# Three input projections by seven block products in place of eight, and modulations computed in other phases

## The chip, the cores and the metric

The program runs on one core of a Trainium2 chip, in one launch. The metric is the device time of that core in microseconds. The kernel before takes 2531.38 us in the median of three runs (2527.74 to 2532.80). The profile and the trace come from one more execution of 2533.03 us, whose first and last instructions lie 2531.3 us apart (the span); all times below are counted from the first instruction of the span. TensorE is named PE in the rows, VectorE DVE, ScalarE ACT, GpSimd POOL and SyncE, which issues the transfers, SP.

## The reference

Two layers on a stream of 512 tokens with 1024 features, plus 256 context tokens. Each layer is half an FFN, a token mixer (HGRN in layer 0, a gated MLP over chunks in layer 1), and half an FFN. Every part is modulated before it and normalised behind it:

```python
def swiglu(h, w_in, w_out):
    gate, up = jnp.split(h @ w_in, 2, axis=-1)
    return (jax.nn.silu(gate) * up) @ w_out

def macaron_half_ffn(x, m, k, w_in, w_out, g, b):
    return post_norm_update(x, 0.5 * swiglu(modulate(x, m, k), w_in, w_out), m, k, g, b)

def modulate(x, m, k):
    return x * (1 + m[..., 3 * k + 1, :]) + m[..., 3 * k, :]

def post_norm_update(x, y, m, k, g, b):
    return layer_norm(DN_ALPHA * x + m[..., 3 * k + 2, :] * y, g, b)
```

`m` holds nine vectors of 1024 for each layer, silu(condition) times a matrix of 1024 x 9216. The hidden width of an FFN is 2816, that is 22 slices of 128, and each slice has a gate half and an up half. All of it is float32.

## The kernel before, in words

**Products.** A float32 operand is kept as two parts: a high part that ScalarE rounds off (L130) and a low part that VectorE subtracts (L131). `mm3` (L140 to L144) makes a product of three matmuls: high by high (L142), high by low (L143), low by high (L144). A weight is loaded as a `unit` (L133) of 128 x 1024: a transfer into `raw` (three buffers), then a split into `w` (six buffers).

**An FFN** is an input phase and an output phase. `FeedIn.rest` (L457) goes over the slices of the hidden width. For each it takes two units, gate and up. Each unit is eight slices of the 1024 features, and each slice multiplies a 128 x 128 block of weights with all 512 tokens: 48 matmuls of 512 columns for the pair, into two PSUM banks `psf`. ScalarE then takes silu of the gate bank (L452), VectorE multiplies it with the up bank (L454) to `h`. f0, f2, f3 and f4 are such phases over the 512 tokens, f1 is one over the 256 context tokens (`psf<-xmc`, 256 columns).

**Output and transition.** `OutPhase` multiplies `h`, split into `hs`, with the output weights into the banks `y`, one half of the 1024 features after the other. Behind the second half comes the transition: VectorE adds the residual and takes statistics (`evac`, L293 to L298), normalises (`norm`), TensorE transposes to banks `pt`, the modulation is applied there in place (L334, L336), and a split writes the next operand `xm` (`operand`). While these steps run, the next phase already multiplies its first two pairs, slice by slice, on 256 tokens at a time (`staged`, four units); `rest` does the other 20 pairs. `store` (L284 to L286) then scales each of the four row tiles by the gain row `rg` and adds the offset row `rb`, for one half of the features and then for the other, and writes them to memory; the rows of the second half are loaded over those of the first, once the latter have been used.

**Modulations.** A vector of `m` is eight chunks of 128 x 1024 loaded into `mraw` (two buffers, L170), each with two VectorE operations (`junk<-mraw,srow_x`, L164). They stand in a queue of generators. `mod_step` takes some at certain places of the loops and `made` takes what is missing. (l;ch) below is vector ch of layer l; ch 2, 5 and 8 are gates, written to memory as rows. (0;8) and (1;2) are queued before f2's rest, (1;5), (1;7), (1;6) and (1;8) before f3's.

**Order.** A planner sorts the instructions of each engine's queue by its own estimates; each queue then runs strictly in that order, so that an instruction that waits holds all that stand behind it on its engine. `tc.issue_after` in the transition holds store() back until the last operand's split has been placed. All transfers shown here are issued from one queue, SyncE's. Pools of SBUF tiles are opened and closed from phase to phase; a tile of a new pool may lie over tiles of an old one, and its first writer then waits for the old one's last users.

Of the kernel before, what the change touches and what calls it, by code (L numbers as in the profile page):

```python
# [70 lines left out]
def backbone_kernel(  # L71
# [36 lines left out]

    last = ctx.enter_context(tc.tile_pool(name="last", bufs=1, side="right"))
# [30 lines left out]
    def mm3(ps, a, b, start, stop):  # L140
        (ah, al), (bh, bl) = a, b
        nc.tensor.matmul(ps, ah, bh, start=start, stop=False)  # L142
        nc.tensor.matmul(ps, ah, bl, start=False, stop=False)  # L143
        return nc.tensor.matmul(ps, al, bh, start=False, stop=stop)  # L144
# [83 lines left out]
    class OutPhase:  # L228
# [4 lines left out]
        def __init__(self, hget, nk, units, nt, l, j, cond, yscale, xsrc, scaled, after, xm, xdst, nxt, tail=2):  # L233
            self.hget, self.nk, self.units, self.nt, self.tail = hget, nk, units, nt, tail
            self.l, self.j, self.cond, self.yscale, self.xsrc = l, j, cond, yscale, xsrc
            self.scaled, self.after, self.xm, self.xdst, self.nxt = scaled, after, xm, xdst, nxt
            self.npair, self.bp = nk // 2, None
            self.ys, self.pos = [[], []], [0, 0]

        def operands(self, hf, kk):  # L240
            w = unit(self.units(hf, kk))
            n, hs = self.nt * P, []
            for i in range(2):
                h = self.hget(2 * kk + i)
                if h.dtype != F32R:
                    s = self.bp.tile([P, 2, T], F32R, tag="hs", name="hs", bufs=2 * self.tail)
# [72 lines left out]
        def operand(self, p, kb):  # L319

            o, ks = slice(p * 2 * P, (p + 1) * 2 * P), slice(2 * kb, 2 * kb + 2)
            cols, xm = self.cols, self.xm
            pt = bank("pt").rearrange("p (k t) -> p k t", t=2 * P)
            for i in range(2):
                k = 2 * kb + i
                for t in range(2):
                    nc.tensor.transpose(
                        pt[:, i, t * P : (t + 1) * P], self.xs[2 * p + t][:, k * P : (k + 1) * P], ident
                    )
            for i in range(2):  # L330
                k = 2 * kb + i
                g, b = cols[:, 0, k : k + 1], cols[:, 1, k : k + 1]
                if i:
                    nc.scalar.activation(pt[:, i, :], pt[:, i, :], AF.Identity, scale=g, bias=b)  # L334
                else:
                    nc.vector.tensor_scalar(pt[:, i, :], pt[:, i, :], g, b, ALU.mult, ALU.add)  # L336
            return split(xm[:, 0, ks, o], xm[:, 1, ks, o], pt)

        def run(self, bp, hook=None, nmod=0):
# [21 lines left out]
            for t in range(nt):  # L361
                for h in held:
                    self.part(1, *h, [t])

# [12 lines left out]
            for i in range(len(steps) + 3):  # L377
                if i == 1 and nt > 2:
                    done(1)
                if i:  # L380
                    nxt.ahead(i)
                if i < len(steps):
                    last = self.operand(*steps[i])
                if i >= 3:
                    nxt.staged(*steps[i - 3])
            if self.xdst is not None:
# [22 lines left out]
    class Phase:  # L409
# [6 lines left out]

        @staticmethod
# [10 lines left out]
    class FeedIn(Phase):  # L428


# [18 lines left out]
        def evac(self, hp, psg, psu):  # L449
            n = self.n  # L450
            s = hp.tile([P, T], F32, tag="silu", name="silu", bufs=1)
# [5 lines left out]
        def rest(self, hp, nmod):  # L457
# [12 lines left out]
            for _ in self.later:  # L470
                pass
            return lambda k: self.hs[k]
# [59 lines left out]
    with sbuf(name="hp", bufs=1) as hp, sbuf(name="modp", bufs=1) as modp:  # L532
# [49 lines left out]
        with bpools() as bp:  # L582

            def context_operand():
# [6 lines left out]
                for ch in (5, 7, 6):  # L591
                    queue_mod(modp, srow, 0, ch, ["x"])
# [15 lines left out]
            ).run(bp)  # L608
# [3 lines left out]
    with sbuf(name="hgo", bufs=1) as hgo, ExitStack() as late:  # L612
# [14 lines left out]
        with sbuf(name="hg", bufs=1) as hg:  # L627
# [234 lines left out]
            f2 = FeedIn(0, 1, None, NT)  # L862
# [51 lines left out]
        with bpools() as bp:  # L914
            xm = new_xm(xmp, "xm", T)
            f2.xm = op.xm = xm
            op.run(bp)
# [3 lines left out]
    with sbuf(name="hp2", bufs=1) as hp, sbuf(name="modp2", bufs=1) as modp, bpools() as bp:  # L921
        srow = {"x": silu_row(modp, "x")}
# [4 lines left out]
        f3 = FeedIn(1, 0, xm, NT)  # L927
        OutPhase(
            hget, NF, ffn_units(0, 1), NT, 0, 2, "x", 0.5, lambda t: x2[t], True, (1, 0),
            xm, lambda t: x3[t], f3, tail=3,  # L930
        ).run(bp, None, 1)
        for ch in (5, 7, 6, 8):
            queue_mod(modp, srow, 1, ch, ["x"])
        hget = f3.rest(hp, 1)
# [27 lines left out]
        OutPhase(  # L962
            hget, NF, ffn_units(1, 0), NT, 1, 0, "x", 0.5, lambda t: x3[t], True, (1, 1),
            xm, lambda t: x4[t], first, tail=3,
        ).run(bp, None, 1)
        for ch in (5, 7, 6, 8):
            made((1, ch, "x"))


    with ExitStack() as vhp_stack:  # L970
# [3 lines left out]
        f4 = FeedIn(1, 1, None, NT)  # L974
# [4 lines left out]
        op.bp = bp  # L979
        with sbuf(name="cm", bufs=1) as cm:  # L980
# [6 lines left out]
            for gi in range(NG):  # L987
# [4 lines left out]
                for t in range(NT):  # L992
                    if gi == 0:
                        ps = first.ps[t]
                    else:
                        ps = bank("pscv")
                        cm_tok(ps, xm, ws, t)
                    nc.scalar.activation(vt[:, t, :], ps[:, :GC], AF.Gelu_apprx_tanh)
                    nc.vector.bn_stats(st[t][:, gi, :], vt[:, t, :])
            stat = []  # L1000
# [47 lines left out]
    with sbuf(name="hp4", bufs=1) as hp, bpools() as bp:  # L1048
        hget = f4.rest(hp, 0)
# [82 lines left out]
```

## Time and profile before

| | |
|---|---|
| median of three runs | 2531.38 us (2527.74 to 2532.80) |
| the profiled execution | 2533.03 us |
| its span | 2531.3 us |
| TensorE busy | 2484.4 us, 98% |
| VectorE busy | 1551.8 us, 61% |
| ScalarE busy | 892.1 us, 35% |
| rest of f2, f3, f4 | 1026.7 to 1244.4, 1394.9 to 1612.4, 2184.5 to 2401.9 us |
| first output phase (layer 0, first FFN) | 260 to 373 us |
| HGRN mixer | 608 to 994 us |
| loop of the chunk MLP's gate | 1747 to 1872 us |

In the table of engines the first number is the busy time, then its share of the span and the instructions. A row of the groups gives line, engine, operation, output<-inputs, shape and count, then the busy time, the mean ns of one, the idle time of the engine just before them and what ended most of it. A row of the timeline is start, length, engine, line, operation, and in brackets the idle time just before with its releaser; xN behind it joins N rows that follow one another. A row of the windows gives the stretch, its length, then busy time and starts of each engine, the granted clock of TensorE (1.00 is full), the busy share of the DMA engines and GB/s. Matmuls overlap, so the distance of their starts, not their listed duration, is what one costs in a full queue.

### The profile page before, as it was taken

The numbers are of one execution on the slowest core, as the hardware profiler recorded it, in microseconds if no ns is written. First come the engines' busy times: TensorE is split into PE (matmuls) and PEld (weight loads), VectorE is DVE, ScalarE is ACT, GpSimd is POOL, SyncE is SP. The second block draws the span as 40 slices with busy tenths as digits, with TensorE's granted clock in tenths as the row PEclk, the third lists the DMA queues.
The fourth block names the chain that finished last, engine by engine and source line by source line (L and its number), as shares of the span: only waits on it lengthen the run. The fifth ranks groups of instructions, "written<-read, shape, count | busy, mean of one in ns | idle before, by whom it ended". The sixth has DMA issues, their size and how long they took to land.

```text
span 2531.3 us, 31944 instructions
## 1 busy us (share of the span) xinstructions
PE 2484.4 (98%) x12527; PEld 2130.6 (84%) x12527; DVE 1551.8 (61%) x2773; ACT 892.1 (35%) x1227; POOL 45.9 (2%) x82
## 2 busy tenths in 40 slices
PE   7999999999999999999999999999999999999998
PEld 5888789988788888888888888888998888888887
DVE  7987668575888886766356432357376356632255
ACT  4222335463445442322243322344232233422241
POOL 0000000000000000000000000000000000000001
PEclk9999999999999999999999999999999999999999
DMA  8878436655521113787232522223443222532221
GB/s 325 287 251 273 154 104 208 197 191 192 193 83 59 59 59 121 253 276 256 96 102 85 185 93 99 99 86 123 160 139 101 83 92 92 189 103 97 95 93 57
DMA packets 111144, 367.70 MB, mean 145 GB/s; under 512 B 12760, under 2 KB 16016, under 8 KB 110992
## 3 DMA queue, kind: packets, MB, share of 16 engines
q1 hardware_dynamic: 110992, 365.65, 42.9%
q8 instruction: 98, 1.61, 0.3%
q14 instruction: 54, 0.44, 0.1%
HBM read 352.99 MB, written 12.61 MB: 144 GB/s over the span
## 4 chain that ended last, share of the span: by engine, by line
PE 74%; DVE 14%; DMA 7%; issue 2%; ACT 2%; POOL 1%; SPq 0%; DVEq 0%; POOLq 0%
PE psf L143 12%; PE psf L144 12%; PE psf L142 11%; PE y L144 8%; PE y L142 8%; PE y L143 8%; DMA mraw<-in_mod_w 6%; DVE junk L164 3%; DVE w L131 2%; PE pscv L143 2%; PE pscv L144 2%; PE pscu L143 2%; PE pscu L142 2%; PE pscv L142 2%; PE pscu L144 2%
## 5 line engine op out<-in xcount | busy, mean ns | idle before, releaser
L131 DVE TENSOR_TENSOR w<-raw,w 128x1024 fp32r<-128x1024 f32 (+1 forms) x458 | 550.2, 1204 | 323.2 <-ACT w L130 321.3
L130 ACT ACTIVATE w<-raw 128x1024 fp32r<-128x1024 f32 (+1 forms) x458 | 473.5, 1039 | 456.2 <-PE psf L144 217.9
L142 PE MATMUL psf<-xm,w 128*128 128x512 f32 (+1 forms) x1504 | 565.9, 378 | 18.4 <-ACT xm L130 17.9
L143 PE MATMUL psf<-xm,w 128*128 128x512 f32 (+1 forms) x1504 | 567.6, 378 | 2.0 <-DVE xm L131 2.0
L144 PE MATMUL psf<-xm,w 128*128 128x512 f32 (+1 forms) x1504 | 567.1, 377 | 2.2 <-DVE w L131 2.2
L144 PE MATMUL y<-w,hs 128*128 128x512 f32 x984 | 383.7, 390 | 2.2 <-DVE hs L131 2.2
L142 PE MATMUL y<-w,hs 128*128 128x512 f32 x984 | 383.7, 390 | 0.0
L143 PE MATMUL y<-w,hs 128*128 128x512 f32 x984 | 383.3, 390 | 0.0
L142 PEld LDWEIGHTS psf<-xm,w 128*128 128x128 f32 x1504 | 283.7, 189 | 71.7 <-ACT xm L130 18.9
L144 PEld LDWEIGHTS psf<-xm,w 128*128 128x128 f32 x1504 | 285.2, 190 | 54.9 <-DVE w L131 3.6
L143 PEld LDWEIGHTS psf<-xm,w 128*128 128x128 f32 x1504 | 285.4, 190 | 54.2 <-DVE xm L131 3.5
L131 DVE TENSOR_TENSOR hs<-h,hs 128x512 fp32r<-128x512 f32 (+1 forms) x220 | 138.4, 637 | 174.7 <-ACT hs L130 174.7
L130 ACT ACTIVATE hs<-h 128x512 fp32r<-128x512 f32 (+1 forms) x220 | 129.3, 589 | 281.0 <-PE y L144 256.9
L164 DVE SCALAR_TENSOR_TENSOR junk<-mraw,srow_x 128x512 bf16<-128x512 f32 x256 | 168.0, 688 | 89.5 <-DMA mraw<-in_mod_w 88.9
L144 PEld LDWEIGHTS y<-w,hs 128*128 128x128 f32 x984 | 185.1, 188 | 41.2 <-DVE hs L131 2.6
L142 PEld LDWEIGHTS y<-w,hs 128*128 128x128 f32 x984 | 185.1, 188 | 38.6
L143 PEld LDWEIGHTS y<-w,hs 128*128 128x128 f32 x984 | 185.1, 188 | 38.3
L452 ACT ACTIVATE silu<-psf 128x512 f32<-128x512 f32 (+1 forms) x110 | 60.9, 554 | 387.5 <-PE psf L144 224.9
L454 DVE TENSOR_TENSOR h<-psf,silu 128x512 f32<-128x512 f32 (+1 forms) x110 | 69.8, 635 | 115.2 <-PE psf L144 111.4
L142 PE MATMUL psf<-xmc,w 128*128 128x256 f32 x352 | 99.8, 283 | 0.0
L144 PE MATMUL psf<-xmc,w 128*128 128x256 f32 x352 | 99.6, 283 | 0.0
L143 PE MATMUL psf<-xmc,w 128*128 128x256 f32 x352 | 99.6, 283 | 0.0
(204 smaller groups left out, 3193.2 us busy)
## 6 DMA issues: line engine op xcount, KB each, us to landing
raw<-in_ffn_w_in SPq DMA_DIRECT2D x220, 512.0 KB, 3.5
mraw<-in_mod_w SPq DMA_DIRECT2D x144, 512.0 KB, 4.4
raw<-in_ffn_w_out SPq DMA_DIRECT2D x110, 512.0 KB, 3.2
raw<-in_hg_wf SPq DMA_DIRECT2D x32, 512.0 KB, 3.3
raw<-in_cm_wv SPq DMA_DIRECT2D x32, 384.0 KB, 3.7
raw<-in_cm_wu SPq DMA_DIRECT2D x24, 512.0 KB, 3.4
raw<-in_cm_w_out SPq DMA_DIRECT2D x24, 512.0 KB, 3.2
x<-x SPq DMA_DIRECT2D x40, 256.0 KB, 3.6
```

The lines of the kernel that those rows point to most:

```text
L130: nc.scalar.activation(dst_hi, src, AF.Copy)
L131: return nc.vector.tensor_tensor(dst_lo, src, dst_hi.bitcast(F32), ALU.subtract)
L142: nc.tensor.matmul(ps, ah, bh, start=start, stop=False)
L143: nc.tensor.matmul(ps, ah, bl, start=False, stop=False)
L144: return nc.tensor.matmul(ps, al, bh, start=False, stop=stop)
L164: nc.vector.scalar_tensor_tensor(junk, w[:, c], 1.0, s[:, c], ALU.mult, ALU.mult, dst[:, i : i + 1])
L452: nc.scalar.activation(s[:, :n], psg[:, :n], AF.Silu)
L454: nc.vector.tensor_tensor(h[:, :n], psu[:, :n], s[:, :n], ALU.mult)
```

## The change

The class `FeedSums` takes the place of `FeedIn` for f2, f3 and f4. The first two pairs stay as they were. For the other 20 the product of a pair is seen as a product of 2 x 2 blocks: weights by gate and up and by lower and upper half of the features, tokens by feature half and by token half (256). Seven products of sums of blocks are made in place of eight: 7 x 4 slices x 3 = 84 matmuls of 256 columns for a pair.

```diff
+    class FeedSums(FeedIn):
+        nsilu = 2
+        def enter(self):
+            fp = self.place.enter_context(swap("sums"))
+            self.f5, self.f6, self.f4, self.f7 = (
+                fp.tile([P, 2, KD // 2, 2 * P], F32R, name=f"f{i}") for i in (5, 6, 4, 7)
+            )
...
+        def sums(self):
+            def add(dst, x, y):
+                for j in range(2):
+                    a, b = self.blocks[x[0], x[1] + j], self.blocks[y[0], y[1] + j]
+                    nc.vector.tensor_tensor(a, a, b, ALU.add)
+                    ks = slice(2 * j, 2 * j + 2)
+                    split(dst[:, 0, ks, :], dst[:, 1, ks, :], a)
+            add(self.f4, (0, 0), (1, 0))
+            add(self.f5, (1, 0), (1, 2))
+            add(self.f6, (1, 2), (0, 0))
+            add(self.f7, (0, 2), (1, 2))
...
+        def rest(self, hp, bp, nmod=0):
...
+            for f in range(len(self.hs), NF):
+                g = wpool.tile([P, D], F32, tag="raw", name="raw", bufs=3)
+                nc.sync.dma_start(g, self.src(2 * f))
+                u = hp.tile([P, D], F32, tag="rawu", name="rawu", bufs=2)
+                nc.sync.dma_start(u, self.src(2 * f + 1))
+                e = bp.tile([P, D], F32, tag="x", name="x", bufs=NT)
...
+                wg = weights(g)
+                nc.vector.tensor_tensor(e[:, lo], g[:, lo], u[:, lo], ALU.subtract)
+                nc.vector.tensor_tensor(u[:, lo], u[:, hi], u[:, lo], ALU.subtract)
+                nc.vector.scalar_tensor_tensor(e[:, hi], u[:, lo], -1.0, g[:, lo], ALU.mult, ALU.subtract)
+                we = weights(e)
+                nc.vector.scalar_tensor_tensor(g[:, lo], g[:, hi], -1.0, e[:, hi], ALU.mult, ALU.subtract)
+                wu = weights(u)
+                w4 = weights(g, K2)
+                pc, pe, pa = bank("psc"), bank("pse"), bank("psa")
+                sc = hp.tile([P, 4, N2], F32, tag="sc", name="sc", bufs=2)
+                def kept(i, ps, scale=1.0):
+                    nc.scalar.activation(sc[:, i, :], ps[:, :N2], AF.Copy, scale=scale)
+                product(pc, wg, 0, b11, True, True)
+                kept(0, pc)
+                product(pe, we, 0, self.f5, True, True)
+                kept(1, pe)
+                product(pc, we, K2, self.f6, False, True)
+                kept(2, pc)
+                product(pa, wg, K2, b21, True, True)
+                product(pc, wu, 0, self.f4, False, True)
+                kept(3, pc, -1.0)
+                product(pe, wu, K2, self.f7, False, True)
+                product(pc, w4, 0, b22, False, True)
+                s = hp.tile([P, T], F32, tag="silu", name="silu", bufs=self.nsilu)
+                h = hp.tile([P, T], F32, tag="h", name="h", bufs=NF)
+                nc.vector.tensor_tensor(s[:, :N2], pa[:, :N2], sc[:, 0, :], ALU.add)
+                nc.scalar.activation(s[:, :N2], s[:, :N2], AF.Silu)
+                nc.vector.tensor_tensor(h[:, N2:], sc[:, 3, :], sc[:, 1, :], ALU.subtract)
+                nc.vector.tensor_tensor(h[:, :N2], pe[:, :N2], sc[:, 2, :], ALU.add)
+                nc.scalar.activation(s[:, N2:], pc[:, :N2], AF.Silu, scale=-1.0)
+                nc.vector.tensor_tensor(h, h, s, ALU.mult)
```

`product` is four slices of `mm3` on 256 columns. The sums over the tokens' blocks (`sums`, into f4 to f7) are made once a phase, in the transition ahead of store(). For this `operand` writes the modulated block to SBUF (`bw`, or tiles `h` not yet used) and not back into the bank. The sums and combinations of weights are new work of VectorE, the four copies `kept` new work of ScalarE. The tile `e` takes buffers of the row tiles `x`, the load of `u` has a pool tile `rawu` of its own, and the tiles of `hs` go into a pool at the other end of SBUF.

The modulations move: (0;8) and (1;2) are queued behind (0;6) in the context's stage, the four of f3 run in the gate loop of the chunk MLP.

```diff
-                for ch in (5, 7, 6):
-                    queue_mod(modp, srow, 0, ch, ["x"])
+                for l, ch in ((0, 5), (0, 7), (0, 6), (0, 8), (1, 2)):
+                    queue_mod(modp, srow, l, ch, ["x"])
...
-        queue_mod(modp, srow, 0, 8, ["x"])
-        queue_mod(modp, srow, 1, 2, ["x"])
-        hget = f2.rest(hp, 2)
+        hget = f2.rest(hp, bp)
...
-        for ch in (5, 7, 6, 8):
-            queue_mod(modp, srow, 1, ch, ["x"])
-        hget = f3.rest(hp, 1)
+        hget = f3.rest(hp, bp)
...
+        modp = early.enter_context(swap("modp3"))
+        srow = {"x": silu_row(modp, "x")}
+        for ch in (5, 7, 6, 8):
+            queue_mod(modp, srow, 1, ch, ["x"])
...
+                    mod_step(1)
                     nc.scalar.activation(vt[:, t, :], ps[:, :GC], AF.Gelu_apprx_tanh)
```

**Where the order moves.** Line numbers of the changed kernel are larger, by 4 in the helpers: L135 is the low part of a split, L168 a modulation's `junk`, L291 and L292 are the row operations of store(), L481 is `h` of the staged pairs.

First place: VectorE at the start of f2's rest. Before, two units (`w_9449`, `w_9479`) are split among the last operands, ahead of the stores; the last rows of store() and what follows them read:

```order
L285 SCALAR_TENSOR_TENSOR x_8881<-rb_9409,x_8881 128x512
L285 SCALAR_TENSOR_TENSOR x_8884<-rb_9409,x_8884 128x512
L131 TENSOR_TENSOR w_9527<-raw_9525,w_9527 128x1024
L131 TENSOR_TENSOR w_9557<-raw_9555,w_9557 128x1024
L131 TENSOR_TENSOR w_9603<-raw_9601,w_9603 128x1024
L454 TENSOR_TENSOR h_9441<-psf_9159,silu_9439 128x512
```

Now, where `w_9613` (wg) alone is split ahead of the stores and `w_9619` is we:

```order
L292 SCALAR_TENSOR_TENSOR x_9011<-rb_9576,x_9011 128x512
L481 TENSOR_TENSOR h_9602<-psf_9298,silu_9600 128x512
L481 TENSOR_TENSOR h_9606<-psf_9300,silu_9604 128x512
L570 TENSOR_TENSOR x_9612<-raw_9608,rawu_9610 128x512
L571 TENSOR_TENSOR rawu_9610<-rawu_9610 128x512
L572 SCALAR_TENSOR_TENSOR x_9612<-rawu_9610,raw_9608 128x512
L570 TENSOR_TENSOR x_9733<-raw_9729,rawu_9731 128x512
L574 SCALAR_TENSOR_TENSOR raw_9608<-raw_9608,x_9612 128x512
L135 TENSOR_TENSOR w_9619<-x_9612,w_9619 128x1024
```

The first pair's second weight tile now stands behind the stores and behind the combinations. SyncE's queue at the same place, with the waits (DMAHW are transfers that must have landed):

```order
L293 DMA x2_84<-x_9008 128x512 [waits DMAHW1_49,DVE_49]
L293 DMA x2_84<-x_9011 128x512 [waits DMAHW2_49,DVE_49]
L561 DMA rawu_9610<-in_ffn_w_in 128x1024 [waits DMAHW3_49,DMAHW2_49,DMAHW4_49,DMAHW1_49,DMAHW5_49,DMAHW0_49,DMAHW7_49,PE_49,Pool_49]
L561 DMA rawu_9731<-in_ffn_w_in 128x1024
L561 DMA rawu_9852<-in_ffn_w_in 128x1024 [waits DMAHW3_49,DVE_49]
```

The first load of u stands behind the last store of the eight, and waits for the transfers on seven of the eight counters; f4 has the same, while f3's loads of u stand in the output phase before it.

Second place: VectorE in the first output phase, behind the last `junk` of (0;6). Before:

```order
L177 TENSOR_REDUCE dot_4392<-acc_x_3828 128x8
L188 SCALAR_TENSOR_TENSOR mc_0_6_x_4394<-dot_4392,mbT_81 128x8
L131 TENSOR_TENSOR w_2237<-raw_2235,w_2237 128x1024
L454 TENSOR_TENSOR h_2043<-psf_2016,silu_2041 128x512
L131 TENSOR_TENSOR w_2272<-raw_2270,w_2272 128x1024
L131 TENSOR_TENSOR hs_2166<-h_618,hs_2166 128x512
L131 TENSOR_TENSOR hs_2169<-h_702,hs_2169 128x512
```

Now, with five chunks of (0;8) ahead of the same `hs` and two between each pair of them and the next:

```order
L168 SCALAR_TENSOR_TENSOR junk_4685,acc_x_4400<-mraw_4681,srow_x_100 128x512
L135 TENSOR_TENSOR hs_2169<-h_618,hs_2169 128x512
L135 TENSOR_TENSOR hs_2172<-h_702,hs_2172 128x512
L135 TENSOR_TENSOR w_2310<-raw_2308,w_2310 128x1024
L168 SCALAR_TENSOR_TENSOR junk_4726,acc_x_4400<-mraw_4724,srow_x_100 128x512
L168 SCALAR_TENSOR_TENSOR junk_4728,acc_x_4400<-mraw_4724,srow_x_100 128x512
L168 SCALAR_TENSOR_TENSOR junk_4755,acc_x_4400<-mraw_4753,srow_x_100 128x512
L168 SCALAR_TENSOR_TENSOR junk_4757,acc_x_4400<-mraw_4753,srow_x_100 128x512
L135 TENSOR_TENSOR hs_2208<-h_786,hs_2208 128x512
```

All 16 chunks of (0;8) and (1;2) stand there, the last ahead of the ninth pair of `hs`.

More of the change, by code (lines that the diff above doesn't have):

```diff
@@ L107, in sbuf, with swap @@
             p.fill()
+    def swap(name, bufs=1):
+        return sbuf(name=name, bufs=bufs, side="right", reuse_waits="tile")
     last = ctx.enter_context(tc.tile_pool(name="last", bufs=1, side="right"))
@@ L363, in run @@
                     self.part(1, *h, [t])
+            self.held.close()
+            if self.release:
+                self.release()
+            if nxt is not None:
+                nxt.enter()
             def done(p):
@@ L385, in run @@
                     nxt.staged(*steps[i - 3])
+            nxt.sums()
             if self.xdst is not None:
@@ L607, in backbone_kernel @@
                 xmc, None, hv,
-            ).run(bp)
+            ).run(bp, None, 1)
+            for l, ch in ((0, 8), (1, 2)):
+                made((l, ch, "x"))
     with sbuf(name="hgo", bufs=1) as hgo, ExitStack() as late:
```

105 lines of the change are left out of this document (82 added, 23 removed).

## The prediction

> **What bounds the kernel now.** I read the page's table of engines first, then the busy time by windows for the stretches that the change touches.
>
> ```profile
> PE 2484.4 (98%) x12527; PEld 2130.6 (84%) x12527; DVE 1551.8 (61%) x2773; ACT 892.1 (35%) x1227; POOL 45.9 (2%) x82
> ```
>
> ```profile
> core 0: us, PE busy (x) PEld busy (x) DVE busy (x) ACT busy (x) POOL busy (x), PEclk, DMA share, GB/s
> 399.00:514.00 115.00, 115.00 (x961) 115.00 (x960) 73.14 (x93) 52.87 (x72) 0.00 (x0) 1.00 0.67 220
> 1026.70:1244.40 217.70, 217.70 (x963) 180.04 (x962) 134.57 (x282) 58.99 (x72) 0.00 (x0) 1.00 0.71 238
> 1394.90:1612.40 217.50, 217.50 (x962) 180.03 (x961) 73.50 (x77) 57.55 (x69) 0.00 (x0) 1.00 0.36 120
> 2184.50:2401.90 217.40, 217.40 (x961) 180.02 (x960) 74.81 (x78) 58.42 (x71) 0.00 (x0) 1.00 0.36 125
> ```
>
> TensorE works 98% of the span. The last three rows are the rests of f2, f3 and f4, 20 pairs each: no gap, at full clock, about 961 starts of 512 columns, so 217.4/961 = 226.2 ns from start to start. The first row is the context input projection, 256 columns: 115.00/961 = 119.7 ns. That is the price of the new products' matmuls, measured in this kernel. (A listed duration overlaps its neighbours and would price a 256-column matmul too high.) So anything that shortens TensorE's queue counts in full, and any wait of TensorE's costs in full.
>
> **The products.** A pair was 2 units x 8 slices x 3 = 48 matmuls of 512: 48 x 226.2 = 10.86 us. It becomes 7 products x 4 slices x 3 = 84 of 256: 84 x 119.7 = 10.05 us. That is 0.80 us a pair, 7.4% and not an eighth: the two pitches fit 13.2 ns + 0.416 ns a column, and 36 more matmuls pay the fixed part once more (0.48 us). Over 60 pairs: **-48.2 us**.
>
> The Trainium skill, "TensorE: Matmul & The Clock Gate", section "Back-to-back issue gap", gives N/2.4 + 2.5 ns for a warm matmul by itself, 109.2 and 215.8 ns here. By that a pair would gain 1.19 us and the three phases 71 us; the rows above show 10 ns more for each matmul, and I go by the rows.
>
> **The side engines in the steady state.**
>
> ```profile
> L131 DVE TENSOR_TENSOR w<-raw,w 128x1024 fp32r<-128x1024 f32 x43 | 52.6, 1225 | 93.8 <-ACT w L130 93.8
> L454 DVE TENSOR_TENSOR h<-psf,silu 128x512 f32<-128x512 f32 x21 | 14.5, 690 | 46.2 <-PE psf L144 46.2
> ```
>
> ```profile
> L130 ACT ACTIVATE w<-raw 128x1024 fp32r<-128x1024 f32 x42 | 44.3, 1056 | 72.6 <-PE psf L144 68.8 <-DMA raw<-in_ffn_w_in 3.8
> L452 ACT ACTIVATE silu<-psf 128x512 f32<-128x512 f32 x21 | 12.6, 598 | 79.5 <-PE psf L144 77.2 <-DVE h L454 2.4
> ```
>
> Vector work of a new pair: three splits of 1024 (3 x 1.225), one of 512, four weight combinations of 512 and one product of 512 (6 x 0.690), three operations of 256 (0.35 to 0.69 each, I take 0.42): 9.1 us, less than the 10.05 of TensorE. Scalar: 3 x 1.056 + 0.598 and six of 256 (0.30 to 0.60, I take 0.40): 6.2 us. Both fit, so I cost them at nothing; the cover is thin in one place, the third rival. The modulation work that leaves f2 and f3 (134.57 against 73.50 us of vector time in the rows above) frees no TensorE time, since TensorE was full there anyway.
>
> **The three entries into the products.** This term decides. At an entry TensorE has the first product's weight (a split ahead of the stores), 12 matmuls = 1.44 us of work. The second needs the weight `we`, a split of e = g - u. In VectorE's queue that split stands behind: the sums (8 additions and 8 splits of 512, new), the 16 row operations of store(), two h, and the combinations. Before, two whole units, 10.9 us of TensorE work, were split ahead of the same stores. At f2 this ran so (VectorE, then SyncE, then ScalarE):
>
> ```profile
> 1017.18 0.69 DVE L131 TENSOR_TENSOR xm<-pt,xm 128x512 fp32r<-128x512 f32 x1 [0.18 <-ACT xm L130]
> ...
> 1020.19 1.29 DVE L284 SCALAR_TENSOR_TENSOR x<-x,rg 128x512 f32<-128x512 f32 x2
> 1021.40 1.29 DVE L285 SCALAR_TENSOR_TENSOR x<-rb,x 128x512 f32<-128x512 f32 x2
> 1025.17 2.50 DVE L284 SCALAR_TENSOR_TENSOR x<-x,rg 128x512 f32<-128x512 f32 x4 [2.48 <-DMA rg<-in_ln_g]
> 1027.92 2.50 DVE L285 SCALAR_TENSOR_TENSOR x<-rb,x 128x512 f32<-128x512 f32 x4 [0.25 <-DMA rb<-in_ln_b]
> 1030.34 3.49 DVE L131 TENSOR_TENSOR w<-raw,w 128x1024 fp32r<-128x1024 f32 x3
> ```
>
> ```profile
> 1021.51 0.33 SPq L225 DMA_DIRECT2D rg<-in_ln_g  x1
> ...
> 1028.64 2.13 SPq L286 DMA_DIRECT2D x<-x  x4
> ```
>
> ```profile
> 1032.67 1.28 ACT L452 ACT_TABLE_LOAD   x1 [4.97 <-DMA x<-x]
> ```
>
> ```profile
> raw<-in_ffn_w_in SPq DMA_DIRECT2D x220, 512.0 KB, 3.5
> ```
>
> Read off: a row operation of 512 follows the last by 0.61 us (four in 2.50); the second half of the stores waits for its row of gains 25.17 - 21.48 = 3.7 us after the last use of the first; the first reader of the reused buffers ran 32.67 - 30.42 = 2.25 us after the last store operation; a weight lands 3.5 us after issue.
>
> f2, with these steps: the last operand split at 1018.9 (1.1 later, since sums now stand between); 14 rows to the last use of the first gains, 0.65 each: 1028; gains 1031.7; the second half, whose offsets come later still: 1037.8; stores landed 1040.1. The load of u goes into a new pool over memory that these stores (and others) still read, so SyncE holds it until then (the order with its waits, above): landed 1043.6. Three combinations: 1045.4; ScalarE's half of the split 1046.5, VectorE's 1047.7. TensorE wants it at 1026.71 + 1.44 = 1028.2. **Stall 19 us.**
>
> f3 and f4 begin from these rows:
>
> ```profile
> 1385.37 0.69 DVE L131 TENSOR_TENSOR xm<-pt,xm 128x512 fp32r<-128x512 f32 x1 [0.19 <-ACT xm L130]
> ...
> 1388.38 1.28 DVE L284 SCALAR_TENSOR_TENSOR x<-x,rg 128x512 f32<-128x512 f32 x2
> ...
> 1393.18 2.50 DVE L284 SCALAR_TENSOR_TENSOR x<-x,rg 128x512 f32<-128x512 f32 x4 [2.31 <-DMA rg<-in_ln_g]
> ```
>
> ```profile
> 2175.00 0.69 DVE L131 TENSOR_TENSOR xm<-pt,xm 128x512 fp32r<-128x512 f32 x1 [1.24 <-ACT xm L130]
> ...
> 2178.01 1.28 DVE L284 SCALAR_TENSOR_TENSOR x<-x,rg 128x512 f32<-128x512 f32 x2
> ...
> 2182.82 2.50 DVE L284 SCALAR_TENSOR_TENSOR x<-x,rg 128x512 f32<-128x512 f32 x4 [2.32 <-DMA rg<-in_ln_g]
> ```
>
> f3: last split 1386.5, 13 rows of 0.61 to 1394.4, gains 3.5 later (before, 1393.18 - 1389.66), 8 rows to 1402.8. Its u is loaded early, only e's tile waits for one store: 1403. Four rows, two splits: 1407.7 against 1394.9 + 1.4 = 1396.3: **11 us**. f4, with the load behind the stores again: 2176.1, 2184.0, 2187.6, 2192.5, 2194.8, u landed 2198.3, `we` 2202.4 against 2185.9: **17 us**. Sum **+47 us**. Bounds: without the load behind the stores f2 and f4 are 13.8 and 10.7, sum 36; with additions at their full 0.69 and the load as slow as the modulations' (4.4 below), some 60.
>
> **The clock after a wait.** The one long wait in an FFN before shows its price:
>
> ```profile
> 271.24 0.39 PE L143 MATMUL y<-w,hs 128*128 128x512 f32 x1
> 273.86 0.79 PE L144 MATMUL y<-w,hs 128*128 128x512 f32 x1 [2.23 <-DVE hs L131]
> 274.45 0.63 PE L142 MATMUL y<-w,hs 128*128 128x512 f32 x1
> 274.88 0.63 PE L143 MATMUL y<-w,hs 128*128 128x512 f32 x1
> ```
>
> After it the start-to-start is 0.43 for some 3 us, 1.6 us lost. Three entries: **+5 us** (3 to 6).
>
> **The modulations.** (0;8) and (1;2), 16 chunks, go into the queue that ran through f0, and in the new order they stand in VectorE's queue of the first output phase, two chunks ahead of every pair of hs.
>
> ```profile
> L164 DVE SCALAR_TENSOR_TENSOR junk<-mraw,srow_x x42: 681/689/694, 208.3 to 269.2; 128x512 bf16<-128x512 f32 x42
> ```
>
> ```profile
> 268.59 0.69 DVE L164 SCALAR_TENSOR_TENSOR junk<-mraw,srow_x 128x512 bf16<-128x512 f32 x1 [0.59 <-DMA mraw<-in_mod_w]
> ...
> 273.12 1.29 DVE L131 TENSOR_TENSOR hs<-h,hs 128x512 fp32r<-128x512 f32 x2
> ```
>
> ```profile
> mraw<-in_mod_w SPq DMA_DIRECT2D x144, 512.0 KB, 4.4
> ```
>
> 21 chunks in 20 intervals from 208.3 to 268.6: 3.0 us a chunk, by the load into two buffers (4.4 us) and not by the arithmetic. Already the wait at 271 is hs behind the last chunk. With 16 more the last ends at 269.8 + 48 = 317.8 and the hs of the ninth pair at 319.4. TensorE had begun that pair at 273.9 + 1.6 + 6 x 5.43 = 308. **+11 us** (18 if hs and chunks do not overlap, 4 at 2.4 us a chunk). In the HGRN phase the next modulations start earlier, as they no longer wait for a new pool, and TensorE's longest wait there stands behind that work:
>
> ```profile
> PE ptk L763 <- ACT X L747: 5.1, 1, 5.1
> ```
>
> I take **-5 us** (0 to -8). The 32 chunks of f3 go to the gate loop of the chunk MLP (127 us, VectorE 63.97 busy, TensorE full): 32 x 3.0 = 96 fit; nothing, up to 8 if a weight split falls behind one.
>
> **Sum.** -48.2 + 47 + 5 + 11 - 5 = +10 on the profiled execution's 2533.03, which is 1.65 over the median of 2531.38: about 2542.
>
> **Rivals.** *The entries cost no more than before*: the new rows run in gaps of TensorE's that exist anyway. Then -48.2 + 11 - 5: 2489, faster. For it: TensorE hardly waited at these places before. Against: then it had 10.9 us of split weights, now 1.44, and each step of the chain has a measured duration; one mechanism alone turns the result, the place of `we` behind the stores, and below 37 us for the three entries the sum goes under zero.
>
> *Shorter entries*: the loads of u do not wait for the stores (36 us instead of 47) and the modulations run at 2.4 us (4 instead of 11): 2524. For it: the eight chunks of one modulation in the HGRN phase came at that pace, 7 intervals in 16.8 us:
>
> ```profile
> 620.31 0.69 DVE L164 SCALAR_TENSOR_TENSOR junk<-mraw,srow_x 128x512 bf16<-128x512 f32 x1 [3.15 <-DMA mraw<-in_mod_w]
> ...
> 637.15 0.69 DVE L164 SCALAR_TENSOR_TENSOR junk<-mraw,srow_x 128x512 bf16<-128x512 f32 x1 [0.72 <-DMA mraw<-in_mod_w]
> ```
>
> Against: the wait stands in the order.
>
> *Each pair waits for a copy*: products 3, 5 and 7 go on adding in a bank that ScalarE must copy first, with one product (1.44 us) between at the narrowest. A copy of 256 is 0.3 to 0.6, so it decides once ScalarE is late by 0.5 to 0.8, in a split of 1.056 for instance. At 0.5 us a pair: +30, 2572. Against: ScalarE is used to 62%.
>
> **Chances.** Forecast 0.50, own range 2530 to 2560; entries free 0.10; shorter entries 0.20; copies 0.20. A measurement of this kernel can tell 0.2%, 5 us, from no change: below 2526.3 lie all of the first rival, two thirds of the second and little of the forecast, 0.25; between 2526.3 and 2536.4 the rest of the second and a part of the forecast, 0.17; above, 0.58. The range leaves out the first rival and the worst of the third: 2500 to 2572.
>
> **What would show it.** In the new profile: 256-column products start every 119.7 ns in runs without gaps (else the first term falls); three single waits of TensorE at the start of the rests, of 19, 11 and 17 us, released by the split of `we`, with the stores and the load of u before them in the chain; VectorE's junk rows reach to about 318 us and the first output phase ends 11 us later; short waits of 0.2 to 0.6 us at every pair would speak for the copies. The forecast is wrong if the three waits sum to less than 37 us or the rests hold gaps.

## The result, and the profile after

The changed kernel takes 2561.7 us in the median of four runs (2558.97 to 2565.84), the kernel before 2531.73 (2527.74 to 2532.80): 30 us slower, a ratio of 1.0123 with a 95% interval of 1.0104 to 1.0142. The forecast was 2542, so the sign was right and the size was a third of what came. The profiled execution is the lowest of the four, 2558.97 us with a span of 2557.2; its span lies 25.9 above that of before, and the rest of this section divides those 25.9 us.

From the page of the changed kernel, the engines:

```profile
PE 2447.0 (96%) x14687; PEld 2202.1 (86%) x14687; DVE 1896.8 (74%) x3361; ACT 1097.1 (43%) x1671; POOL 47.5 (2%) x82
```

VectorE has 345 us more work and ScalarE 205, but neither is the bound. Now the stretches that the change touches, in the new kernel: the rests of f2, f3 and f4, the first output phase and the gate loop of the chunk MLP.

```profile
1034.70:1257.70 223.00, 203.79 (x1683) 203.26 (x1682) 179.82 (x259) 122.40 (x208) 0.00 (x0) 0.95 0.39 130
1406.20:1621.90 215.70, 204.01 (x1683) 203.70 (x1682) 179.71 (x256) 120.24 (x206) 0.00 (x0) 0.97 0.37 124
2206.90:2428.00 221.10, 204.02 (x1682) 203.49 (x1682) 179.49 (x256) 122.40 (x208) 0.00 (x0) 0.96 0.39 130
260.00:382.40 122.40, 111.26 (x481) 91.55 (x481) 84.07 (x154) 44.72 (x61) 0.00 (x0) 0.94 0.57 178
1755.90:1892.40 136.50, 129.57 (x723) 127.70 (x722) 100.85 (x228) 42.74 (x66) 4.08 (x6) 0.97 0.77 256
```

And the last two of them in the kernel before, with as many matmuls (482 starts against 481, and 723):

```profile
260.00:373.00 113.00, 110.77 (x482) 91.18 (x481) 65.53 (x89) 44.78 (x61) 0.00 (x0) 0.98 0.37 123
```

```profile
1746.80:1871.70 124.90, 124.90 (x723) 124.90 (x722) 62.36 (x93) 43.51 (x66) 4.08 (x6) 1.00 0.47 155
```

The three rests last 659.8 us where they lasted 652.6: +7.2, in spite of the smaller number of blocks. The first output phase lasts 9.4 longer, the gate loop 11.6: 6.9 of the latter are gaps of TensorE's (136.50 - 129.57), the other 4.7 are its busy time on as many starts (129.57 against 124.90) at a granted clock of 0.97 in place of 1.00. Everything from the context's FFN to the start of f2's rest gives 1.4 back (it begins 9.4 late, the rest 8.0 late), the transitions about 1 more.

What TensorE waited for in the new kernel (total, times, longest):

```profile
PE pse L146 <- ACT w L134: 47.8, 3, 19.2
...
PE y L148 <- DVE hs L135: 11.1, 1, 11.1
PE pscv L147 <- DVE w L135: 6.8, 3, 2.9
PE ptk L902 <- ACT X L886: 6.0, 1, 6.0
```

There are three waits of 47.8 us together for the second product's weight (19.2 at f2, 11.7 at f3, 17.0 at f4), one of 11.1 for hs, three of 6.8 in the gate loop, and one of 6.0 in the HGRN mixer. The wait for hs stands ahead of the first of the `hs` rows shown in the order, behind the five chunks:

```profile
282.67 0.80 PE L148 MATMUL y<-w,hs 128*128 128x512 f32 x1 [11.14 <-DVE hs L135]
```

The entry of f2, in TensorE's timeline, and the chain behind it on VectorE, SyncE and ScalarE:

```profile
1036.18 0.28 PE L148 MATMUL psc<-xm,w 128*128 128x256 f32 x1
1055.62 0.58 PE L146 MATMUL pse<-f,w 128*128 128x256 f32 x1 [19.16 <-ACT w L134]
1056.00 0.41 PE L147 MATMUL pse<-f,w 128*128 128x256 f32 x1
1056.21 0.41 PE L146 MATMUL psc<-f,w 128*128 128x256 f32 x1
...
1058.94 0.28 PE L148 MATMUL pse<-f,w 128*128 128x256 f32 x1
1059.06 0.28 PE L148 MATMUL psc<-f,w 128*128 128x256 f32 x1
```

```profile
1041.75 1.29 DVE L291 SCALAR_TENSOR_TENSOR x<-x,rg 128x512 f32<-128x512 f32 x2 [5.81 <-DMA rg<-in_ln_g]
...
1045.37 1.29 DVE L292 SCALAR_TENSOR_TENSOR x<-rb,x 128x512 f32<-128x512 f32 x2
1051.06 1.29 DVE L481 TENSOR_TENSOR h<-psf,silu 128x512 f32<-128x512 f32 x2 [4.40 <-ACT silu L479]
1052.33 0.69 DVE L570 TENSOR_TENSOR x<-raw,rawu 128x512 f32<-128x512 f32 x1
```

```profile
1043.67 3.33 SPq L293 DMA_DIRECT2D x<-x  x4
1048.94 0.81 SPq L561 DMA_DIRECT2D rawu<-in_ffn_w_in  x2
```

```profile
1049.13 1.28 ACT L479 ACT_TABLE_LOAD   x1 [18.78 <-DMA x<-x]
...
1054.51 1.06 ACT L134 ACTIVATE w<-x 128x1024 fp32r<-128x1024 f32 x1 [2.72 <-DVE x L572]
```

The last row of the stores is done at 1046.7, the load of u is issued at 1048.9 when they have landed, e is begun at 1052.3, its split at 1054.5, and TensorE goes on at 1055.6. The links of the prediction are all there, in its order. One more stands beside them: ScalarE's table load for silu is released by the stores' transfers too, and the two `h` that stand in VectorE's queue ahead of e wait 4.4 us for that silu. They end at 1052.35; the load of u, 3.4 to 3.6 us from issue to landing, ends at about the same time. At f4 the load is the later one, by 0.40 us; at f3 VectorE's rows of the stores run on into e without a wait.

### The profile page after: what moved, and what is told of

Its sections match the earlier page's. It is cut to its first block, busy times and chain, and to the rows that moved or that the text cites. A ratio compares the mean times of both kernels' runs of the same rounds, so it can differ in the third digit from the quotient of the medians.

```text
span 2557.2 us, 37486 instructions
## 1 busy us (share of the span) xinstructions
PE 2447.0 (96%) x14687; PEld 2202.1 (86%) x14687; DVE 1896.8 (74%) x3361; ACT 1097.1 (43%) x1671; POOL 47.5 (2%) x82
## 4 chain that ended last, share of the span: by engine, by line
PE 65%; DVE 18%; DMA 11%; issue 3%; ACT 3%; POOL 1%; SPq 0%; DVEq 0%; POOLq 0%; ACTq 0%
DMA mraw<-in_mod_w 8%; PE y L148 8%; PE y L146 8%; PE y L147 8%; PE psc L146 4%; PE psc L147 4%; PE psc L148 4%; DVE junk L168 4%; PE psf L148 2%; PE psf L147 2%; PE psf L146 2%; PE pse L146 2%; PE pse L148 2%; PE pse L147 2%; DVE w L135 2%
## 5 line engine op out<-in xcount | busy, mean ns | idle before, releaser
L135 DVE TENSOR_TENSOR w<-raw,w 128x1024 fp32r<-128x1024 f32 (+1 forms) x458 | 516.8, 1132 | 141.8 <-ACT w L134 140.4
L134 ACT ACTIVATE w<-raw 128x1024 fp32r<-128x1024 f32 (+1 forms) x458 | 449.0, 983 | 349.8 <-PE y L148 92.1
L148 PE MATMUL y<-w,hs 128*128 128x512 f32 x984 | 384.0, 390 | 11.1 <-DVE hs L135 11.1
L135 DVE TENSOR_TENSOR hs<-h,hs 128x512 fp32r<-128x512 f32 (+1 forms) x220 | 136.4, 635 | 140.8 <-ACT hs L134 140.6
L148 PEld LDWEIGHTS y<-w,hs 128*128 128x128 f32 x984 | 185.2, 188 | 50.2 <-DVE hs L135 11.6
L168 DVE SCALAR_TENSOR_TENSOR junk<-mraw,srow_x 128x512 bf16<-128x512 f32 x256 | 168.1, 687 | 75.9 <-DMA mraw<-in_mod_w 75.8
L146 PE MATMUL psf<-xm,w 128*128 128x512 f32 (+1 forms) x544 | 191.8, 359 | 18.5 <-ACT xm L134 18.0
L148 PE MATMUL psf<-xm,w 128*128 128x512 f32 (+1 forms) x544 | 192.7, 355 | 2.1 <-DVE w L135 2.1
L147 PE MATMUL psf<-xm,w 128*128 128x512 f32 (+1 forms) x544 | 193.1, 356 | 0.8 <-DVE xm L135 0.8
L146 PE MATMUL pse<-f,w 128*128 128x256 f32 x480 | 137.9, 287 | 47.8 <-ACT w L134 47.8
L148 PE MATMUL pse<-f,w 128*128 128x256 f32 x480 | 137.8, 287 | 0.0
L147 PE MATMUL pse<-f,w 128*128 128x256 f32 x480 | 137.4, 286 | 0.0
L146 PE MATMUL psc<-f,w 128*128 128x256 f32 x480 | 136.8, 285 | 0.1
L147 PE MATMUL psc<-f,w 128*128 128x256 f32 x480 | 136.4, 284 | 0.0
L148 PE MATMUL psc<-f,w 128*128 128x256 f32 x480 | 136.2, 284 | 0.0
L146 PE MATMUL psc<-xm,w 128*128 128x256 f32 x480 | 135.8, 283 | 0.0
L147 PE MATMUL psc<-xm,w 128*128 128x256 f32 x480 | 135.8, 283 | 0.0
```

What stands on the lines that cost most here:

```text
L134: nc.scalar.activation(dst_hi, src, AF.Copy)
L135: return nc.vector.tensor_tensor(dst_lo, src, dst_hi.bitcast(F32), ALU.subtract)
L146: nc.tensor.matmul(ps, ah, bh, start=start, stop=False, **kw)
L147: nc.tensor.matmul(ps, ah, bl, start=False, stop=False, **kw)
L148: return nc.tensor.matmul(ps, al, bh, start=False, stop=stop, **kw)
L168: nc.vector.scalar_tensor_tensor(junk, w[:, c], 1.0, s[:, c], ALU.mult, ALU.mult, dst[:, i : i + 1])
```

## The experiments

They ran in three sessions. The kernel before took 2529.9, 2529.2 and 2529.8 us in the median there; ratios are to those runs. The changed kernel was not run again, so a difference from its 2561.7 us is one between sessions, whose kernels before differ by about 2 us.

**All but the products.** The classes of f2, f3 and f4 go back to the old one (f2's line is shown):

```diff
-            f2 = FeedSums(0, 1, None, NT, lambda i: bw.tile([P, 2, 2 * P], F32, name=f"bw{i}"))
+            f2 = FeedIn(0, 1, None, NT)
```

> All of the change but the products: the old input phases for f2, f3 and f4, with the modulations in their new places (and hs in its new pool). Theory (the parts add up, and the moved modulations lose what the new trace shows of them: 9.5 us in the first output phase, 12 in the gate loop of the chunk MLP, 1 won in the HGRN phase): 2531.7 + 20 = 2552 us. Rival (the modulations are hidden, and the waits seen in those places come with the products): 2532 us.

Measured: 2546.76 us (2537.05 to 2552.08), ratio 1.0064 (1.0043 to 1.0085), 17 us slower than before, 20 expected. The waits that the new places cause are there without any product by blocks:

```profile
PE y L148 <- DVE hs L135: 11.7, 1, 11.7
PE ptk L902 <- ACT X L886: 6.4, 1, 6.4
PE pscv L147 <- DVE w L135: 3.8, 3, 3.0
```

The move of the modulations is a loss of its own, and more than half of the total. The runs of this kernel spread by 15 us, more than others, and the profiled execution is the slowest of them, 2552.08.

**Without the moved modulations' work.**

```diff
+        moved = (l, ch) in ((0, 8), (1, 2), (1, 5), (1, 7), (1, 6), (1, 8))
...
-        for f in range(KD):
+        for f in range(0 if moved else KD):
```

The lines left out set the sums of the moved vectors to zero: this kernel leaves out part of the computation and serves for its time alone.

> The changed kernel with the 48 chunks of the six moved modulations left out: their vectors are the bias alone, and nothing is loaded or multiplied for them. Theory: 2561.7 - 20 = 2541 us, with the three waits at the entries unchanged at 19.3, 11.8 and 17.2 us; so the products alone still do not win. Rival (the entries wait because VectorE and SyncE are loaded with modulations elsewhere): the entries shrink by several us and the time falls under 2532.

Measured: 2537.38 us (2532.61 to 2541.29), ratio 1.0031 (1.0019 to 1.0043): still slower than before. The wait for hs is gone, the entries are what they were:

```profile
PE pse L146 <- ACT w L134: 46.9, 3, 19.5
```

So the changed kernel loses 24 us with the modulations' work in its new places, and the products alone lose 8: their 47 us are eaten by the entries. The 24 are not all a price of the move: without that work the context's FFN starts at 380.3 us, 3.8 earlier than before, where TensorE waited 2.2 us for hs already. The two separate losses against before, 17 and 8, make 25 of the 30.

**Two old pairs at each entry.**

```diff
+            for f in range(len(self.hs), len(self.hs) + 2):
+                pss = []
+                for i in range(2):
+                    w = unit(self.src(2 * f + i))
+                    ps = bank("psf")
+                    feat_mm(ps, w, xm, 0, T)
+                    pss.append(ps)
+                self.evac(hp, *pss)
             for f in range(len(self.hs), NF):
```

> The changed kernel, but the first two pairs of each of the three rests are made the old way, by eight blocks, so that 21.8 us of TensorE work with weights split early stand ahead of the first seven-product pair. Theory (the waits at the entries are the only loss of the products): 48.3 us of waits and about 5 of slow clock go, 6 pairs x 0.80 us come: 2561.7 - 48.5 = 2513 us, and no wait over 1 us in the rests. Rival (VectorE carries its backlog from the transition on, with 1 us a pair to spare, and the wait only moves to later pairs): waits of 10 us and more remain in each rest, over 2535 us.

Measured: 2509.3 us (2503.52 to 2511.59), ratio 0.9918 (0.9898 to 0.9938), 4 us from the forecast and faster than before. The three rests hold no wait:

```profile
1037.50:1241.00 203.50, 203.50 (x1612) 199.67 (x1611) 167.99 (x241) 113.41 (x192) 0.00 (x0) 1.00 0.41 138
1389.50:1592.80 203.30, 203.30 (x1611) 199.54 (x1610) 167.90 (x238) 112.02 (x190) 0.00 (x0) 1.00 0.37 126
2175.10:2378.40 203.30, 203.30 (x1611) 199.53 (x1610) 167.17 (x237) 113.44 (x192) 0.00 (x0) 1.00 0.40 137
```

TensorE is busy from the first to the last microsecond at full clock, so VectorE carries no backlog on, and no copy is late: both rivals of that kind fall. The rows also price a pair: (217.5 - 203.4)/18 = 0.78 us.

**The first pair's u in an early buffer.**

```diff
-                u = hp.tile([P, D], F32, tag="rawu", name="rawu", bufs=2)
+                if f == len(self.pss) // 2:
+                    u = wpool.tile([P, D], F32, tag="raw", name="rawf", bufs=3)
+                else:
+                    u = hp.tile([P, D], F32, tag="rawu", name="rawu", bufs=2)
```

> The changed kernel, but the first pair's u is loaded into the raw buffers of the weight pool, which are free early, and not into the new pool that waits for the stores. Theory (the load behind the stores is one link of the chain at f2 and f4): the waits there fall from 19.3 to about 14 and from 17.2 to about 11, f3 stays at 12: 2561.7 - 12 = 2550 us. Rival (VectorE's rows of the stores alone set the end): no change, 2562 us.

Measured: 2551.6 us (2547.28 to 2555.27), ratio 1.0089 (1.0071 to 1.0107), 10 below the changed kernel. At f2 the waits are now

```profile
PE psc L148 <- DVE w L135: 5.3, 1, 5.3
PE pse L146 <- ACT w L134: 3.5, 2, 2.4
```

and at f4 one of 12.9 us. The rests of f2 and f4 are about 8 and 4 us shorter; f3's wait, the control, is 11.4. The load behind the stores was a link, but the test is not as clean as meant: at f2 the planner, once u came early, also put the combinations and the split of we ahead of the stores' second half, so two links were cut there at once (8.8 us instead of the 14 expected). VectorE's rows there:

```profile
1041.81 1.23 DVE L135 TENSOR_TENSOR w<-x,w 128x1024 fp32r<-128x1024 f32 x1 [0.46 <-ACT w L134]
1044.06 1.29 DVE L291 SCALAR_TENSOR_TENSOR x<-x,rg 128x512 f32<-128x512 f32 x2 [1.03 <-DMA rg<-in_ln_g]
```

At f4 the wait stayed 2 us above what was expected. There the first combination, which writes e, waited for the stores although u was there: e takes a buffer of the row tiles x that the stores still read. The prediction counted this link at f3 and not at f4:

```profile
2212.28 0.69 DVE L573 TENSOR_TENSOR x<-raw,rawf 128x512 f32<-128x512 f32 x1 [2.20 <-DMA x<-x]
```

**(0;8) and (1;2) held back.** They are queued after the first output phase, and their loads and vector operations are ordered behind its last weight and its last hs:

```diff
-            nc.sync.dma_start(raw, mod_w[l, ch, f])
-            for c in conds:
-                mod_dot(modp, accs[c][:, f, :], raw, srow[c])
+            with behind((l, ch)):
+                nc.sync.dma_start(raw, mod_w[l, ch, f])
+                for c in conds:
+                    mod_dot(modp, accs[c][:, f, :], raw, srow[c])
...
+            for l, ch in ((0, 8), (1, 2)):
+                held_back[l, ch] = [op.tail_split.ins, op.tail_dma]
+                queue_mod(modp, srow, l, ch, ["x"])
             hget = f1.rest(hp, 1)
```

Here `behind` opens `tc.issue_after` for each instruction in the list.

> The changed kernel, with (0;8) and (1;2) held back: their loads and vector operations are ordered behind the last weight and the last hs of the first output phase, and so run during the context's FFN. Theory (in the changed kernel 16 chunks of 3 us stand between TensorE and hs, and nothing waits for their result so early): the wait at 271 us goes from 11.3 back to about 2.4 us and the time falls by 9.5 us, to 2552. Rival (the chunks only move their cost to the context's FFN, whose VectorE is busy 64%): a wait of the same size there, 2560.

Measured: 2550.2 us (2544.11 to 2552.16), ratio 1.0077 (1.0060 to 1.0094), 11 below the changed kernel. The phase has its old length, and the wait for hs is 2.1 us:

```profile
260.00:373.00 113.00, 110.86 (x483) 91.19 (x482) 65.96 (x91) 44.94 (x61) 0.00 (x0) 0.98 0.42 133
```

**f3's modulations spread over two loops.** One chunk in every second step of the gate loop, the others in the loop of the up products, each ordered behind the weight loaded and split last:

```diff
+            held_back[1, ch] = unit_last
...
-                    mod_step(1)
+                    if t % 2:
+                        mod_step(1)
...
+                    if gi < NG - 1:
+                        mod_step(1)
```

> The changed kernel, with the 32 chunks of f3's modulations spread over the gate loop and the loop of the up products behind it (16 and 16), each ordered behind the weights that were loaded before it. Theory (the gate loop loses 8 to 12 us because SyncE's and VectorE's queues hold weights behind chunks that wait for their two buffers): waits of the gate loop fall under 1 us each, time 2551 us. Rival (the gate loop loses to the DMA load itself): the same waits, now in both loops, 2560.

Measured: 2550.61 us (2548.41 to 2554.30), ratio 1.0085 (1.0069 to 1.0100), 11 below the changed kernel. The gate loop and the loop behind it, of this kernel:

```profile
1764.30:1889.30 125.00, 125.00 (x724) 124.91 (x723) 81.20 (x165) 43.06 (x66) 3.29 (x6) 1.00 0.65 230
1889.30:2054.00 164.70, 163.59 (x818) 138.69 (x817) 115.54 (x203) 45.94 (x62) 2.37 (x3) 1.00 0.45 146
```

The gate loop lasts 125.0 us, as before the change, and the second loop 164.7, where it took 163.8 before and 164.3 in the changed kernel. The transfers did not get quicker: the loads of this loop's weights land after 4.4 us in the changed kernel and after 4.8 here (first the changed kernel's row, then this one's):

```profile
raw<-in_cm_wv SPq DMA_DIRECT2D x24, 384.0 KB, 4.4
```

```profile
raw<-in_cm_wv SPq DMA_DIRECT2D x24, 384.0 KB, 4.8
```

So the usual time of a load is not what was paid. The changed kernel's trace shows what stood ahead of each of its three waits there. The longest, 2.9 us up to 1775.5, had a weight whose load was issued behind a chunk's and landed late, 6.9 us after its issue; SyncE's and ScalarE's rows:

```profile
1766.42 0.33 SPq L174 DMA_DIRECT2D mraw<-in_mod_w  x1
1767.33 0.33 SPq L139 DMA_DIRECT2D raw<-in_cm_wv  x1
```

```profile
1774.19 0.84 ACT L134 ACTIVATE w<-raw 128x768 fp32r<-128x768 f32 x1 [9.16 <-DMA raw<-in_cm_wv]
```

At the other two, ScalarE's half of the weight's split was done, and VectorE's half stood behind a chunk whose load had not landed (ScalarE's, VectorE's and TensorE's rows):

```profile
1835.70 0.85 ACT L134 ACTIVATE w<-raw 128x768 fp32r<-128x768 f32 x1 [0.19 <-PE pscv L148]
1837.13 0.69 DVE L168 SCALAR_TENSOR_TENSOR junk<-mraw,srow_x 128x512 bf16<-128x512 f32 x1 [1.74 <-DMA mraw<-in_mod_w]
...
1839.30 1.82 DVE L135 TENSOR_TENSOR w<-raw,w 128x768 fp32r<-128x768 f32 x2
1840.31 0.44 PE L147 MATMUL pscv<-w,xm 128*128 128x384 f32 x1 [1.34 <-DVE w L135]
```

```profile
1851.95 1.84 ACT L134 ACTIVATE w<-raw 128x768 fp32r<-128x768 f32 x2 [0.60 <-PE pscv L148]
1856.54 0.69 DVE L168 SCALAR_TENSOR_TENSOR junk<-mraw,srow_x 128x512 bf16<-128x512 f32 x1 [3.43 <-DMA mraw<-in_mod_w]
...
1858.85 1.82 DVE L135 TENSOR_TENSOR w<-raw,w 128x768 fp32r<-128x768 f32 x2
1859.86 0.45 PE L147 MATMUL pscv<-w,xm 128*128 128x384 f32 x1 [2.61 <-DVE w L135]
```

So in two of the three waits the order of VectorE's queue held TensorE. The loss is in every kernel that has all 32 chunks in this loop: from the first to the last start of the gate product they take 143.5 to 148.9 us, where the kernel before takes 135.5, the three with spread chunks 135.5 and 135.6, and the one without the chunks' work 135.8. The kernel here halves the rate in this loop and orders each chunk behind the weights at once; which of the two took the 11.6 us away was not taken apart.

**All three repairs.**

> All three repairs together: two old pairs at each entry, (0;8) and (1;2) held back, f3's modulations spread. Theory (the losses add up and each repair takes its own): 2509 - 9.5 - 8 = 2492 us, the best of all kernels. Rival (the repairs overlap, or the planner's order changes elsewhere): 2505 or more.

Measured: 2492.25 us (2487.62 to 2495.28), ratio 0.9850 (0.9832 to 0.9868): 1.5% faster than before and the best of all. The three rests:

```profile
1028.30:1232.20 203.90, 203.59 (x1611) 199.63 (x1611) 168.01 (x241) 113.12 (x192) 0.00 (x0) 1.00 0.41 138
1382.20:1585.50 203.30, 203.30 (x1611) 199.54 (x1610) 167.52 (x237) 112.01 (x190) 0.00 (x0) 1.00 0.37 126
2157.60:2361.70 204.10, 203.60 (x1611) 199.63 (x1611) 167.67 (x238) 113.28 (x192) 0.00 (x0) 1.00 0.40 136
```

They hold 0.8 us of waits in 611. Both of these are waits for a copy, the mechanism of the third rival, which is real but rare:

```profile
PE psc L148 <- ACT sc L603: 0.8, 2, 0.5
```

**Ten old pairs at each entry.** As with two, with 10 in the first line of that diff.

> As the run with two old pairs at each entry, but with ten of the 20 made the old way, so that 24 more pairs pay for eight blocks. Theory (a seven-product pair saves the 0.80 us that the two measured matmul pitches give): 19 us slower than with two, 2528 us. Rival (a pair saves the 1.19 us of the formula with 2.5 ns for each matmul): 29 us slower, 2538. Rival (each pair loses to copies or to VectorE, and saves less): under 12 us slower, 2521.

Measured: 2528.43 us (2526.09 to 2532.62), ratio 0.9996 (0.9987 to 1.0006). Against two old pairs the ratios differ by 0.0078, 19.7 us for 24 pairs: 0.82 us a pair, and by the two intervals some 0.6 to 1.05. The measured pitches gave 0.80. An estimate by the formula of the Trainium skill's "TensorE: Matmul & The Clock Gate", section "Back-to-back issue gap", would be 1.19, and this run does not bear that out for these float32 products.

**The new places, repaired, without products.** This is the kernel of the first experiment with both repairs of the modulations' order.

> The old input phases for f2, f3 and f4, with the modulations in their new places and both repairs of their order (held back behind the first output phase; spread over the two loops of the chunk MLP). No products by blocks. Theory (the move costs only through the queues, and the seven products with two old pairs are worth 54 x 0.80 = 43 us): the time of the kernel before, 2530 us, and so about 39 to 43 above the kernel with all three repairs. Rival (the repairs win something of their own, as f2's and f3's rests are relieved): 2520 us or less.

Measured: 2529.96 us (2528.75 to 2535.87), ratio 1.0001 (0.9991 to 1.0011): the time of before. With these repairs the move is free, and wins nothing. The kernel with all repairs lies 38 us below this one, 5 less than 54 x 0.80. One place for these 5 is in the traces: its first output phase still has two waits for hs, 2.4 and 1.6 us, against one of 1.5 here, and its context's FFN starts at 387.1 us and not at 381.9. Why is open.

## Why the prediction was right and wrong

**The sign and the reason** were right: the products save what the two pitches say, and the entries take it back. Term by term, predicted and then measured on the profiled pair:

| term | predicted | measured |
|---|---|---|
| 60 pairs by seven products | -48.2 | -47 (0.78 a pair, from the kernel with two old pairs) |
| three waits at the entries | 19 + 11 + 17 = 47 | 19.2 + 11.7 + 17.0, 47.8 in all |
| slow clock behind them | +5 | +6.5, a remainder (rests 659.8, less 605.5 for 60 pairs at that saving, less 47.8) |
| (0;8), (1;2) in the first output phase | +11 | +9.4 |
| earlier modulations in the HGRN phase | -5 | -1.4 |
| f3's modulations in the gate loop | 0 (to 8) | +11.6 |
| transitions | 0 | -1 |
| sum | +10 | +26 |

**The steps that failed** are two. The first is "32 x 3.0 = 96 fit; nothing, up to 8 if a weight split falls behind one". I compared the sum of the chunks with the length of the loop. The loop, in which VectorE was half idle before (62.36 of 124.90 us), loses 11.6 us with all 32 chunks among its weights in the queues, and none with half of them, each behind the weights. What the bound of 8 names did happen, at two of three waits; the slow clock behind the waits, 4.7 of the 11.6, was not counted here at all. I had read the order of the queues for the first output phase and did not read it for the gate loop. The second is "-5 us" in the HGRN phase: the wait that it was to remove is 6.0 us in the changed kernel and 5.1 before, and between 3.7 and 9.9 in the other kernels that move the modulations; the earlier start did not shorten it. Why that wait is as long as it is stays open. These two make 15 of the 16 us that the profiled pair is off. The other 4 us between 26 and the 30 of the medians lie in the spread of the runs: the profiled execution of before, 2533.03, lies above all its runs, that of the changed kernel below its others.

**Two terms that fit, and how.** The 47 us of the entries came out although the wait of the two `h` for ScalarE's silu was not in the chain; that it ended together with the load of u, and added nothing, was luck. In the first output phase the prediction put the loss at the ninth pair of hs, from the last chunk. The 16 chunks did come every 3.0 us (269.2 to 314.1), but nearly all of the loss is one wait at the first of these hs, up to 282.7: it stood behind the five chunks ahead of it. The bound of 4 us at 2.4 us a chunk is not what that sum gives (269.8 + 38.4 + 1.6 - 308 = 1.8).

**The rivals.** *The entries cost no more than before* fell with the three waits themselves. *Shorter entries* fell as well: the load of u did wait for the stores at f2 and f4, and the chunks came at 3.0 us. *Each pair waits for a copy* fell with the rests of the kernel with two old pairs, TensorE busy 203.5 of 203.5 us; the most that was seen of it in the rests is 0.8 us, with all three repairs. The true time lay on the side of that last rival, but not by its mechanism.

**What I would have needed** is the same reading of the order at every place to which work was moved: in VectorE's and SyncE's order, which weight or hs stands behind the moved rows, and when TensorE wants it.

## What to carry to other kernels

A change that saves work on a full engine counts in full only from the point at which its inputs can be ready. Look at the first instance after each transition: how much of the engine's work is prepared ahead of the slow rows in the queues, before and after. Here the weights split ahead of the stores used to cover 10.9 us of TensorE's work and then covered 1.44, and keeping the old form for two of twenty pairs turned +1.2% into a gain. Work moved into a loop with idle time is free only if it does not hold up what that loop needs next; the free time of the engine does not show that, the order of the queues does.

## What the runs showed of the hardware

A wait of TensorE's of 11.7 to 19.2 us cost little more in clock than one of 2.2. After the wait of 2.23 us in the kernel before, nine intervals of 512 columns took 3.7 us (273.86 to 277.58) instead of 9 x 0.226 = 2.0, so 1.7 were lost. After the wait of 19.2 us the matmuls of 256 columns stood 0.38 and 0.21 us apart at first, at a granted clock of 0.52 (1055.6 to 1059.0); the 14 intervals from 1055.62 to 1058.94 took 3.3 us instead of 14 x 0.12 = 1.7, so 1.6 were lost. Read in the same way, f3 lost 2.2 (20 intervals in 4.6 us) and f4 2.0 (18 in 4.2): 5.8 for the three, near the remainder of 6.5 in the table.

A gain row of the stores landed 5.5 us after its issue at f2 (issued at 1036.26, VectorE resumed at 1041.75), when it was issued right behind three stores; in the kernel before it was 3.7 us, behind two (issued at 1021.51, resumed at 1025.17). Why is open. The stores' end, predicted for 1037.8 + 8.0, as f2's rest begins 8.0 late, came at 1046.7, so the error was under 1 us.
